# Eight chunks of the modulation as one-column products on TensorE, all in the first block

## The chip, the cores and the metric

One Trainium2 chip, one core of it. The metric is the device time of one execution in microseconds. The five engines (TensorE, VectorE, ScalarE, GpSimd and SyncE) each have their own instruction queue, taken in order, and meet by semaphores. Nearly all plain loads and stores are issued from SyncE's queue.

## What is computed

A streaming-encoder block over 1024 tokens of 1024 channels, in fp32. A vector `c` gives, by one matrix `w_ada` (1024 x 6144), six rows of 1024: shift, scale and gate of each of two sub-layers.

```python
c_act = jax.nn.silu(c)
mod = c_act @ w_ada[l] + b_ada[l]
shift1, scale1, gate1, shift2, scale2, gate2 = jnp.split(mod, 6, axis=-1)
n = modulate(rms_norm(h, g_norm1[l]), shift1, scale1)      # n * (1 + scale) + shift
...                                     # w_in, convolution branch, spatial-gating branch, merged
h = h + gate1[:, None, :] * (merged @ w_out[l])
n2 = modulate(rms_norm(h, g_norm2[l]), shift2, scale2)
h = h + gate2[:, None, :] * peer(n2, w_query[l], sub_keys[l], expert_u[l], expert_v[l])
return rms_norm(h, g_final)
```

`peer` picks 16 of 16384 single-neuron experts for each of 8 heads and each token.

## The kernel before

The 1024 tokens are eight tiles of 128, taken in three blocks of 3, 2 and 3 tiles (`BLOCKS`). For each block `front` (L993) runs the first sub-layer, the second norm and the expert scores. Its products are all of 128 x 128 weights against the block's tokens, in three fp32r passes (high x high, low x high, high x low), so 24 matmuls of 384 columns for a product of the first block. The order in the first block: the loop over eight channel groups with the products `w_av`, `w_ag` (both in `glu`) and `w_u`, and the small mixing products; a loop with `w_gb` and `w_sgu`; a loop with `w_ga`; the convolution's end (L1056); a loop with `w_conv`; then `w_out` (`products_t`), the residual with `gate1`, the second norm and its transposition (`n2_T`, L1098), the next block's `w_v` product (`v_of`) and the query products. Each weight tile of 512 KB is loaded (`raw`), split into a high and a low half by ScalarE and VectorE (`whi`, `wlo`), and the low half is stored to DRAM for the next blocks. The depthwise convolution (31 taps) is a chain of multiply-adds on VectorE, done in the background (`conv`, L899). After the three blocks come the experts, some for all tokens of five tiles as dense products and some by gathered rows.

A planner (`Plan`, L61) writes the order out by hand while the program is built. It keeps an estimated clock for each engine. Between matmul groups `tick` (L263) steps generators whose due time has come: tasks first, then background work by its class. Background work is stepped only while VectorE's clock is less than `lead` ahead of TensorE's, unless it was added with `free=True`. `drain` (L284) steps named generators until they end, wherever TensorE then stands.

The modulation is made in twelve chunks of 512 columns: chunk `ch` is half `ch % 2` of row `ch // 2`. A chunk is four loads of 512 KB (`aw`, a ring of `NST` = 4 buffers shared with `st` tiles that are used much later). Chunks 0 to 3 are made before the first block, half on TensorE (stationary: one column of `cT`, moving: 512 columns of `w_ada`) and half on VectorE. Chunks 4 to 11 are made by `ada` (L742) in the background: eight VectorE operations over 128 partitions into `acc`, one TensorE product with a matrix of ones that adds the partitions and puts the row on all of them, the bias, and for shift2 and scale2 four transposes into `mcol`. The rows go to `rows_d` in DRAM. `rest_of_ada` (L1233) makes three groups of it: (4, 5), gate1; (6, 7, 8, 9), shift2 and scale2; (10, 11), gate2. `front` drains the first at L1073, ahead of the residual, and `n2_T` the first two at L1102, ahead of its transposes. `zeros` (L554) clears 16 MB in DRAM in the same time, a megabyte at a time, when the planner's DMA clock is idle. PSUM has five tiles in `psp` that all products take in turn.

Of the kernel before, what the change touches and what calls it, by code (L numbers as in the profile page):

```python
# [7 lines left out]
F32 = mybir.dt.float32  # L8
# [5 lines left out]
OP = mybir.AluOpType  # L14
AX = mybir.AxisListType

P = 128
D = 1024
J = D // P
# [16 lines left out]
NST = 4  # L36
# [265 lines left out]
def build(ctx, tc, I, O):  # L302
    nc = tc.nc
    out = O["out"]
    pl = Plan(nc)
# [3 lines left out]
    rows_d = dram.tile([4, D], F32, name="rows_d")  # L309
# [13 lines left out]
    ident = cst.tile([P, P], F32, name="ident")  # L323
# [280 lines left out]
    tp = fctx.enter_context(tc.tile_pool(name="tp", bufs=4))  # L604
    sctx = ExitStack()
    gsb = sctx.enter_context(tc.tile_pool(name="gsb", bufs=1, side="right"))
# [3 lines left out]
    def psum():  # L610
        return psp.tile([P, 512], F32, name="ps", tag="ps")

    def cload(name, shape):
        t_ = fc.tile(shape, F32, name=name)
        pl.load(t_, I[name])
        return t_


    def flat(w):
        return w.rearrange("p j c -> p (j c)")  # L620
# [83 lines left out]
    ada_todo = []  # L704
# [30 lines left out]
    cT = cload("cT", [P, J])  # L735
    ones = fc.tile([P, P], F32, name="ones")
    nc.vector.memset(ones, 1.0)
    pl.act(cT, cT, AF.Silu)
    mcol = fc.tile([P, 4, J], F32, name="mcol")


    def ada(ch):  # L742
        which, half = divmod(ch, 2)
        acc = tp.tile([P, 512], F32, name="acc", tag="acc", bufs=3)
        row = tp.tile([P, 512], F32, name="row", tag="acc", bufs=3)
        pl.load(row, I["b_ada"][ch:ch + 1, :].partition_broadcast(P))
        hs = slice(half * 512, (half + 1) * 512)
        raw = []

        def fetch(jq):  # L750
            if jq < 4:
                raw.append(gsb.tile([P, 2, 512], F32, name="aw", tag="st", bufs=NST))
                pl.load(raw[jq], I["w_ada"][ch, jq])

        for jq in range(3):
            fetch(jq)
        for j in range(J):
            w = raw[j // 2]
            yield pl.ready(w)
            if j == 0:  # L760
                pl.ts(acc, w[:, 0, :], cT[:, 0:1], None, OP.mult)
            else:
                pl.stt(acc, w[:, j % 2, :], cT[:, j:j + 1], acc, OP.mult, OP.add)
            if j % 2:
                fetch(j // 2 + 3)
        yield pl.ready(acc)
        ps = psum()
        pl.mm(ps, ones, acc, True, True)
        f = pl.tt(row, row, ps, OP.add)
        yield f  # L770
        if which in (3, 4):
            pt = psum()
            for a in range(4):
                pl.tr(pt[:, a * P:(a + 1) * P], row[:, a * P:(a + 1) * P], ident)
            src = pt.rearrange("p (a b) -> p a b", a=4)[:, :, 0]
            js = slice(half * 4, half * 4 + 4)
            if which == 3:
                pl.vcopy(mcol[:, 2, js], src)
            else:
                pl.stt(mcol[:, 3, js], src, 1.0, cols[:, 6, js], OP.add, OP.mult)  # L780
        if which == 4:
            pl.load(acc, I["g2"][half:half + 1, :].partition_broadcast(P))
            yield pl.ready(acc)
            yield pl.stt(acc, row, 1.0, acc, OP.add, OP.mult)
            pl.load(rows_d[2:3, hs], acc[0:1, :])
        else:
            r = {2: 0, 5: 1, 3: 3}[which]
            pl.load(rows_d[r:r + 1, hs], row[0:1, :])

    held = []  # L790

    def to_T(xn, hi, lo, sl, ca, cb, spill=None):

        while len(held) > 1:
            yield max(pl.now, pl.t["dve"]) + 0.1
        held.append(1)
        nf = tp.tile([P, J, P], F32, name="nf", tag="t4k", bufs=2)
        yield pl.ready(xn)
        for b in range(2):
            pt = psum()  # L800
            for a in range(4):
                j = b * 4 + a
                pl.tr(pt[:, a * P:(a + 1) * P], xn[:, j * P:(j + 1) * P], ident)
            for a in range(4):
                j = b * 4 + a
                src = pt[:, a * P:(a + 1) * P]
                if pl.t["dve"] + DLAG < pl.t["act"]:
                    pl.ts(nf[:, j, :], src, mcol[:, ca, j:j + 1], mcol[:, cb, j:j + 1], OP.mult, OP.add, 1.0)
                else:
                    pl.act(nf[:, j, :], src, AF.Identity, bias=mcol[:, cb, j:j + 1], scale=mcol[:, ca, j:j + 1])  # L810
            js = slice(b * 4, b * 4 + 4)
            f = pl.acopy(hi[:, js, sl], nf[:, js, :])
        yield f
        if spill is not None:
            pl.load(spill, nf)
        f = pl.sub(lo[:, :, sl], nf, hi[:, :, sl].bitcast(F32))
        held.pop()
        yield f

    def norm_tile(x, o):  # L820
        yield pl.ready(x)
        sq = tp.tile([P, D], BF16, name="sq", tag="so", bufs=2)
        ss = tp.tile([P, 1], F32, name="ss", tag="ss")
        yield pl.act(sq, x, AF.Square, accum_out=ss)
        r = tp.tile([P, 1], F32, name="rstd", tag="rstd", bufs=4)
        yield pl.act(r, ss, AF.Sqrt, bias=eps, scale=1.0 / D)
        yield pl.recip(r)
        yield pl.act(o, x, AF.Copy, scale=r)
# [18 lines left out]
    def big(tag, dt=F32):  # L847
        pool = ap if tag[1] in "hl" else ap1
        return pool.tile([P, J, NM], dt, name=tag, tag=tag)
# [143 lines left out]
    def front(b, nn, v, cv):  # L993
# [76 lines left out]
        pl.flush()  # L1070


        pl.drain(ada_todo[:1])  # L1073
        nn = []
        if nxt:
            ng = pl.task(norm_in(*nxt, b + 1, nn))
# [21 lines left out]
        def n2_T(t):  # L1098
            yield pl.ready(h1[:, t, :])
            pl.load(h1_d[tk(t), :], h1[:, t, :])  # L1100
            yield from norm_tile(h1[:, t, :], xn[:, t, :])
            pl.drain(ada_todo[:2])  # L1102
            yield from to_T(xn[:, t, :], n2h, n2l, slice(t * P, (t + 1) * P), 3, 2,
                            n2t_d[:, :, tk(t)] if t0 + t < NDT else None)

# [24 lines left out]
        n2h, n2l = pair(b)  # L1130
        xn = big("sga").rearrange("p j n -> p (j n)").rearrange("p (t d) -> p t d", d=D)
        n2g = [pl.task(n2_T(t)) for t in range(nt)]
        for g in n2g:
            g[3] = -1
# [48 lines left out]
    cols = cload("cols", [P, 9, J])  # L1183
# [7 lines left out]
    f = next(ng)  # L1191

    for tag in ("zc", "sga", "gh", "gl", "nh", "nl"):
        w = big(tag, F32R if tag[1] in "hl" else F32).rearrange("p j n -> p (j n)")
        for a in range(w.shape[1] // D):
            i = len(pieces)
# [11 lines left out]
    for ch in range(4):  # L1208
        acc = tp.tile([P, 512], F32, name="acc", tag="acc", bufs=3)
        ps = psum()  # L1210
        for j in range(J):
            w = pieces[4 * ch + j // 2][:, j % 2 * 512:(j % 2 + 1) * 512]
# [9 lines left out]
        row = tp.tile([P, 512], F32, name="row", tag="acc", bufs=3)  # L1222
# [7 lines left out]
    pl.drain([ng])  # L1230
    v = v_of(*nn, BLOCKS[0][1])

    def rest_of_ada(i, chs):  # L1233
        while any(pl.alive(g) for g in ada_todo[:i]):
            yield pl.now + 1.0
        for ch in chs:
            yield from ada(ch)

    for i, chs in enumerate(((4, 5), (6, 7, 8, 9), (10, 11))):
        ada_todo.append(pl.add(rest_of_ada(i, chs)))  # L1240
    sct = Scatter(gsb, pgp)

    scs = []
# [31 lines left out]
    for b, blk in enumerate(BLOCKS):  # L1275
        nn, v, cv = front(b, nn, v, cv)
# [43 lines left out]
    class Rows:  # L1320
# [7 lines left out]
        def fetch(self):  # L1328
            k = next(self.order, None)
            if k is not None:  # L1330
                self.raw[k] = dq1.tile([P, D], F32, name="raw", tag="raw", bufs=NRAW)
                x, i = k
                pl.load(self.raw[k], flat(I["uT"][i]) if x == "u" else I["v"][i * P:(i + 1) * P, :])
# [132 lines left out]
    for j in range(J):  # L1466
        tag = ("hh", "hl")[j % 2]
# [35 lines left out]
    half = (len(seq) + 1) // 2  # L1503
# [215 lines left out]
```

## Time and profile before

| | us |
|---|---|
| median of 3 runs | 3412.43 |
| lowest and highest | 3403.44, 3421.6 |
| the profiled execution | 3407.5 |
| its span | 3405.0 |

The profile is of one execution, from the hardware's profiler. TensorE's records are its matmuls, and their ends are modelled, so a busy TensorE is not one at its peak; the intervals between starts tell the rate. An fp32 product shows as two matmul records, an fp32r one as one. The granted clock is 1.0 at 2.4 GHz and 0.5 at 1.2 GHz.

### The profile page before, as it was taken

Reading aid. Unit: us, or ns where it says so; the run is one execution under the profiler, and the core shown is the slowest. Engines: PE = TensorE matmul, PEld = TensorE weight load, DVE = VectorE, ACT = ScalarE, POOL = GpSimd, SP = SyncE. Lnnn points to the kernel's source line nnn. Section 1 sums busy time; section 2 is a strip of 40 time slices with the busy share of each in tenths; the row PEclk is TensorE's granted clock in tenths of the full one; section 3 lists DMA queues with packets and bytes.
Section 4 is the critical chain, followed back from the end, with each engine's and each line's share of the span. In section 5 each row is a group of like instructions: output and inputs, shape, how many; then the busy total and the mean of one; then the engine's idle time right before and its main releaser. Section 6 shows DMA issues by size and latency. Waiting matters only on the chain.

```text
span 3405.0 us, 49599 instructions
## 1 busy us (share of the span) xinstructions
PE 3108.5 (91%) x17857; PEld 2831.7 (83%) x17857; DVE 2886.0 (85%) x5888; ACT 1159.3 (34%) x2042; POOL 1471.6 (43%) x1293
## 2 busy tenths in 40 slices
PE   7979858888899989899999999999999999999991
PEld 4969748787799988798999999989999988888980
DVE  4889647777898977659999999989998989999997
ACT  4223433335643365653222222222223222222221
POOL 0000000027899983001555566145514656666663
PEclk9989979999899999899999999999999999999995
DMA  7979678889898877666999999599957999999997
GB/s 249 304 240 308 230 279 291 275 301 287 259 310 233 247 189 244 235 243 200 333 356 337 330 346 361 172 331 340 352 198 284 352 326 350 362 341 358 349 345 272
DMA packets 441830, 997.41 MB, mean 293 GB/s; under 512 B 69384, under 2 KB 212616, under 8 KB 441584
## 3 DMA queue, kind: packets, MB, share of 16 engines
q1 hardware_dynamic: 294000, 591.01, 50.4%
q0 software_dynamic: 147584, 403.24, 34.4%
q8 instruction: 140, 2.29, 0.3%
q14 instruction: 106, 0.87, 0.1%
HBM read 880.32 MB, written 113.79 MB: 292 GB/s over the span
## 4 chain that ended last, share of the span: by engine, by line
PE 53%; DMA 18%; DVE 17%; issue 6%; ACT 3%; POOL 1%; SPq 1%; DVEq 0%; ACTq 0%; POOLq 0%
PE ps L144 18%; PE pa L144 16%; PE pk L144 9%; PE pr L144 6%; PE pg L144 4%; DVE ya L174 4%; DMA raw<-in_v 4%; DMA w<-in_v,e 2%; DVE scr L174 2%; DMA w<-in_u,e 1%; DVE wlo L161 1%; DMA raw<-in_w_out 1%; DVE zc L174 1%; ACT whi L203 1%; DVE vl L161 1%
## 5 line engine op out<-in xcount | busy, mean ns | idle before, releaser
L575 POOL DMA_INDIRECT g_a<-gate,at x256 | 458.7, 1792 | 819.5 <-DVE at L168 744.1
L1420 POOL DMA_INDIRECT w<-in_u,e x384 | 485.7, 1265 | 554.9 <-DVE scr L174 254.3
L1420 POOL DMA_INDIRECT w<-in_v,e x384 | 492.1, 1281 | 336.5 <-DVE ya L174 247.1
L144 PE MATMUL pa<-n2h,uh 128*128 128x320 f32 x2016 | 625.0, 310 | 12.3 <-ACT ge L195 10.1
L144 PE MATMUL pa<-n2l,uh 128*128 128x320 f32 x2016 | 625.4, 310 | 0.8 <-DVE n2l L161 0.8
L144 PE MATMUL pa<-n2h,ul 128*128 128x320 f32 x2016 | 625.0, 310 | 0.0
L174 DVE SCALAR_TENSOR_TENSOR ya<-w,aa,ya 128x1024 f32<-128x1024 f32 x381 | 489.1, 1284 | 27.8 <-DMA w<-in_v,e 22.9
L174 DVE SCALAR_TENSOR_TENSOR scr<-w,n 128x1024 bf16<-128x1024 f32 x384 | 469.6, 1223 | 15.8 <-DMA w<-in_u,e 11.2
L203 ACT CAST whi<-raw 128x1024 fp32r<-128x1024 f32 x264 | 276.7, 1049 | 388.7 <-PE ps L144 90.5
L144 PEld LDWEIGHTS pa<-n2h,uh 128*128 128x128 f32 x2016 | 380.5, 189 | 24.5 <-ACT ge L195 12.6
L144 PE MATMUL ps<-nh,whi 128*128 128x384 f32 (+1 forms) x1024 | 351.5, 343 | 42.8 <-DVE z L161 20.0
L144 PEld LDWEIGHTS pa<-n2l,uh 128*128 128x128 f32 x2016 | 380.5, 189 | 11.1 <-DVE n2l L161 1.7
L144 PEld LDWEIGHTS pa<-n2h,ul 128*128 128x128 f32 x2016 | 380.6, 189 | 0.0
L195 ACT ACTIVATE ge<-pa 128x320 f32<-128x320 f32 x249 | 108.7, 436 | 720.6 <-PE pa L144 720.4
L144 PE MATMUL ps<-nh,wlo 128*128 128x384 f32 (+1 forms) x1024 | 343.7, 336 | 7.9 <-DVE wlo L161 7.7
L144 PE MATMUL ps<-nl,whi 128*128 128x384 f32 (+1 forms) x1024 | 343.0, 335 | 1.6 <-DVE nl L161 1.6
L144 PE MATMUL pk<-vh,hh 128*128 128x512 f32 x768 | 299.5, 390 | 0.0
L144 PE MATMUL pk<-vl,hh 128*128 128x512 f32 x768 | 299.3, 390 | 0.0
L144 PE MATMUL pk<-vh,hl 128*128 128x512 f32 x768 | 299.2, 390 | 0.0
L203 ACT CAST hh<-ge 128x320 fp32r<-128x320 f32 x250 | 115.1, 460 | 509.5 <-DVE ge L161 509.5
L144 PE MATMUL ps<-gh,whi 128*128 128x256 f32 (+1 forms) x704 | 224.2, 318 | 20.5 <-ACT gh L203 17.9
L144 PE MATMUL ps<-gh,wlo 128*128 128x256 f32 (+1 forms) x704 | 219.5, 312 | 18.7 <-DMA wlo<-lo_d_w_ag 12.7
(249 smaller groups left out, 6763.3 us busy)
## 6 DMA issues: line engine op xcount, KB each, us to landing
raw<-in_uT SPq DMA_DIRECT2D x128, 512.0 KB, 6.7
raw<-in_v SPq DMA_DIRECT2D x128, 512.0 KB, 7.1
raw<-in_w_q SPq DMA_DIRECT2D x48, 512.0 KB, 4.2
g_b<-st SPq DMA_DIRECT2D x48, 512.0 KB, 4.7
gt<-g_b SPq DMA_DIRECT2D x32, 640.0 KB, 18.7
wlo<-lo_d_w_q SPq DMA_DIRECT2D x33, 512.0 KB, 6.1
g_a<-zt SPq DMA_DIRECT2D x16, 1024.0 KB, 8.2
aw<-in_w_ada SPq DMA_DIRECT2D x32, 512.0 KB, 7.6
```

What stands on the lines that cost most here:

```text
L144: self.nc.tensor.matmul(ps, w, x, start=start, stop=stop)
L161: self.nc.vector.tensor_tensor(out=out, in0=a, in1=b, op=op)
L174: self.nc.vector.scalar_tensor_tensor(out, a, s, b, op0=op0, op1=op1, **kw)
L195: self.nc.scalar.activation(out, a, func, **kw)
L203: self.nc.scalar.copy(out, a)
L575: i = nc.gpsimd.indirect_dma_start(out=g_1, out_offset=bass.IndirectOffsetOnAxis(ap=at[:, k:k + 1], axis=0), in_=gate[:, k:k + 1], in_offs ...
L1420: nc.gpsimd.indirect_dma_start(out=w, out_offset=None, in_=I["v" if ph else "u"], in_offset=bass.IndirectOffsetOnAxis(ap=ra[a][0][:, k:k + ...
```

## The change

`ada` becomes one generator over all eight chunks, added with `free=True`. The next chunk's four loads are issued when the products of the one before are due to be done. A chunk's eight products run on TensorE as one accumulation into one partition of PSUM, with a column of `cT` stationary; VectorE adds the bias to one partition. The four transposes become four products with a one-element operand into four columns of one PSUM tile. The loads of the bias and of `g2` go to one partition instead of all. `front` drains all chunks at L1073, and the drain in `n2_T` is gone.

```diff
-    def ada(ch):
-        which, half = divmod(ch, 2)
-        acc = tp.tile([P, 512], F32, name="acc", tag="acc", bufs=3)
-        row = tp.tile([P, 512], F32, name="row", tag="acc", bufs=3)
-        pl.load(row, I["b_ada"][ch:ch + 1, :].partition_broadcast(P))
...
-        for jq in range(3):
-            fetch(jq)
-        for j in range(J):
-            w = raw[j // 2]
-            yield pl.ready(w)
-            if j == 0:
-                pl.ts(acc, w[:, 0, :], cT[:, 0:1], None, OP.mult)
-            else:
-                pl.stt(acc, w[:, j % 2, :], cT[:, j:j + 1], acc, OP.mult, OP.add)
-            if j % 2:
-                fetch(j // 2 + 3)
-        yield pl.ready(acc)
-        ps = psum()
-        pl.mm(ps, ones, acc, True, True)
-        f = pl.tt(row, row, ps, OP.add)
...
+    def ada(chs):
+        todo = [(ch, jq) for ch in chs for jq in range(4)]
+        raw = {}
+
+        def fetch():
+            if todo:
+                k = todo.pop(0)
+                raw[k] = gsb.tile([P, 2, 512], F32, name="aw", tag="st", bufs=NST)
+                pl.load(raw[k], I["w_ada"][k])
+
+        for _ in range(4):
+            fetch()
+        for ch in chs:
+            which, half = divmod(ch, 2)
+            hs = slice(half * 512, (half + 1) * 512)
+            row = tp.tile([P, 512], F32, name="row", tag="acc", bufs=3)[0:1, :]
+            pl.load(row, I["b_ada"][ch:ch + 1, :])
+            yield max(pl.ready(raw[ch, 3]), pl.ready(row))
+            ps = psum()
+            for j in range(J):
+                pl.mm(ps[0:1, :], cT[:, j:j + 1], raw[ch, j // 2][:, j % 2, :], j == 0, j == J - 1)
+            yield pl.ready(ps[0:1, :])
+            for _ in range(4):
+                fetch()
+            yield pl.tt(row, row, ps[0:1, :], OP.add)
+            if which in (3, 4):
+                pt = psum()
+                for a in range(4):
+                    pl.mm(pt[:, a:a + 1], row[:, a * P:(a + 1) * P], ones[0:1, 0:1], True, True)
...
+            r = {2: 0, 5: 1, 4: 2, 3: 3}[which]
+            pl.load(rows_d[r:r + 1, hs], row)
...
-        pl.drain(ada_todo[:1])
+        pl.drain(ada_todo)
...
-            pl.drain(ada_todo[:2])
...
-    for i, chs in enumerate(((4, 5), (6, 7, 8, 9), (10, 11))):
-        ada_todo.append(pl.add(rest_of_ada(i, chs)))
+    ada_todo.append(pl.add(ada(range(4, 12)), free=True))
```

## Rows read from the trace of the kernel before

**Rows 1.** The page: engines by busy tenths in 40 equal slices of the span
```profile
PE   7979858888899989899999999999999999999991
DVE  4889647777898977659999999989998989999997
```

**Rows 2.** Busy time by stretch: PE, PEld, DVE, ACT, POOL, granted clock, DMA share, GB/s
```profile
88.00:229.00 141.00, 112.42 (x618) 107.70 (x616) 116.51 (x212) 36.97 (x47) 0.00 (x0) 0.90 0.83 269
229.00:350.00 121.00, 116.13 (x607) 109.88 (x608) 109.27 (x178) 41.87 (x58) 0.00 (x0) 0.96 0.89 289
...
446.00:493.00 47.00, 12.12 (x38) 7.42 (x38) 18.92 (x36) 12.03 (x22) 0.00 (x0) 0.54 0.60 224
493.00:516.00 23.00, 20.71 (x84) 15.86 (x84) 12.22 (x17) 10.22 (x16) 0.00 (x0) 0.98 0.95 354
```

**Rows 3.** TensorE's waits at 88-229, 229-360, 446-493, 516-600: total, times, longest
```profile
PE ps L144 <- DVE z L161: 20.0, 2, 13.4
...
PE ps L144 <- ACT gh L203: 9.2, 1, 9.2
...
PE ps L144 <- DVE acc L174: 32.3, 2, 16.8
...
PE ps L144 <- DMA wlo<-lo_d_w_ag: 5.9, 3, 3.8
```

**Rows 4.** Timeline of TensorE, 445 to 493 us: start, duration, instruction, idle before it
```profile
445.67 0.40 PE L144 MATMUL ps<-whi,gl 128*128 128x512 f32 x1
461.63 2.08 PE L144 MATMUL ps<-acc,ones 128*128 128x512 f32 x2 [15.56 <-DVE acc L174]
...
482.38 2.07 PE L144 MATMUL ps<-acc,ones 128*128 128x512 f32 x2 [16.77 <-DVE acc L174]
...
492.78 0.78 PE L144 MATMUL ps<-whi,gh 128*128 128x512 f32 x1
```

**Rows 5.** Timeline of SyncE's queue: loads of the chunks and of weights
```profile
94.97 1.49 SPq L236 DMA_DIRECT2D aw<-in_w_ada  x3
...
101.60 6.25 SPq L236 DMA_DIRECT2D raw<-in_w_av  x1
...
465.60 0.33 SPq L236 DMA_DIRECT2D raw<-in_w_v  x1
...
468.61 2.13 SPq L236 DMA_DIRECT2D aw<-in_w_ada  x4
...
498.27 0.33 SPq L236 DMA_DIRECT2D raw<-in_w_v  x1
```

**Rows 6.** Timeline of TensorE, 28 to 33 us: products of the first four chunks
```profile
28.90 1.05 PE L144 MATMUL ps<-ones,row 1*128 1x1 f32 x8 [0.66 <-ACT row L203]
29.88 2.73 PE L144 MATMUL ps<-nh,cT 128*1 128x512 f32 x6
```

**Rows 7.** Instructions on tile aw: ns min/median/max, first and last start
```profile
L174 DVE SCALAR_TENSOR_TENSOR acc<-aw,cT,acc x56: 743/752/753, 131.6 to 544.9; 128x512 f32<-128x512 f32 x56
...
L166 DVE TENSOR_SCALAR acc<-aw,cT x8: 478/484/488, 131.0 to 522.7; 128x512 f32<-128x512 f32 x8
...
DMA to landing us min/median/max: 6.9/7.6/8.6
```

**Rows 8.** Timeline of TensorE, 83 to 92 us: first and last of 48 matmuls back to back
```profile
83.77 0.34 PE L144 MATMUL ps<-nh,wlo 128*128 128x384 f32 x1
...
91.92 0.34 PE L144 MATMUL ps<-nl,whi 128*128 128x384 f32 x1
```

**Rows 9.** Groups on TensorE, 88 to 229 us: count, busy us, mean ns, idle before
```profile
L144 PE MATMUL ps<-nh,whi 128*128 128x384 f32 x184 | 65.8, 357 | 25.4 <-DVE z L161 20.0 <-ACT whi L203 3.1 <-ACT ts L195 2.1
```

**Rows 10.** Busy time in ten-microsecond stretches, columns as in rows 2
```profile
100.00:110.00 10.00, 5.76 (x30) 5.12 (x29) 2.23 (x7) 1.44 (x2) 0.00 (x0) 0.92 1.03 356
110.00:120.00 10.00, 10.00 (x48) 10.00 (x48) 8.24 (x14) 2.61 (x3) 0.00 (x0) 0.74 0.91 307
```

**Rows 11.** Timeline of TensorE, 338 to 350 us: the convolution's channel norm
```profile
338.56 5.32 PE L144 MATMUL ps<-zc,onesd 128*128 128x384 f32 x16
```

More of the change, by code (lines that the diff above doesn't have):

```diff
@@ L739, in build @@
     mcol = fc.tile([P, 4, J], F32, name="mcol")
-    def ada(ch):
-        which, half = divmod(ch, 2)
-        acc = tp.tile([P, 512], F32, name="acc", tag="acc", bufs=3)
-        row = tp.tile([P, 512], F32, name="row", tag="acc", bufs=3)
-        pl.load(row, I["b_ada"][ch:ch + 1, :].partition_broadcast(P))
[L747 to L753, printed above, removed]
-        for jq in range(3):
-            fetch(jq)
-        for j in range(J):
-            w = raw[j // 2]
-            yield pl.ready(w)
-            if j == 0:
-                pl.ts(acc, w[:, 0, :], cT[:, 0:1], None, OP.mult)
-            else:
-                pl.stt(acc, w[:, j % 2, :], cT[:, j:j + 1], acc, OP.mult, OP.add)
-            if j % 2:
-                fetch(j // 2 + 3)
-        yield pl.ready(acc)
-        ps = psum()
-        pl.mm(ps, ones, acc, True, True)
-        f = pl.tt(row, row, ps, OP.add)
[L770 to L788, printed above, removed]
@@ new lines, in ada @@
+    def ada(chs):
[25 more added lines that the diff above has]
+                    pl.mm(pt[:, a:a + 1], row[:, a * P:(a + 1) * P], ones[0:1, 0:1], True, True)
+                js = slice(half * 4, half * 4 + 4)
+                yield pl.ready(pt)
+                if which == 3:
+                    pl.vcopy(mcol[:, 2, js], pt[:, 0:4])
+                else:
+                    pl.stt(mcol[:, 3, js], pt[:, 0:4], 1.0, cols[:, 6, js], OP.add, OP.mult)
+            if which == 4:
+                g2 = tp.tile([P, 512], F32, name="g2", tag="acc", bufs=3)[0:1, :]
+                pl.load(g2, I["g2"][half:half + 1, :])
+                yield pl.ready(g2)
+                yield pl.stt(row, row, 1.0, g2, OP.add, OP.mult)
+            r = {2: 0, 5: 1, 4: 2, 3: 3}[which]
+            pl.load(rows_d[r:r + 1, hs], row)
@@ L1231, in build @@
     v = v_of(*nn, BLOCKS[0][1])
[L1233 to L1237, printed above, removed]
-    for i, chs in enumerate(((4, 5), (6, 7, 8, 9), (10, 11))):
-        ada_todo.append(pl.add(rest_of_ada(i, chs)))
+    ada_todo.append(pl.add(ada(range(4, 12)), free=True))
     sct = Scatter(gsb, pgp)
```

## Prediction

> **What bounds the kernel now.** I read from the whole to the part. The page's 40 slices first [rows 1]: TensorE is busy to 9 tenths nearly everywhere, and it ends a slice and a half before VectorE does. The weak slices are the first eighteen; the change lies in the first seven (0 to 600 us). What happens there shifts everything that follows, because the later blocks and the experts depend on this one's output. So the question is by how many microseconds the point at 600 us moves.
>
> Then a table by stretch [rows 2]. The first product loop (88 to 229 us) keeps TensorE busy for 112 of 141 us; 229 to 350 has 116 of 121 and ends in a wait of 9.2 us for the convolution's output [rows 3]; and 446 to 493 has 12 of 47, at a mean granted clock of 0.54. That last hole is the largest on TensorE before the end, and the waits name its cause [rows 3]: 32.3 us in two waits for `acc` on VectorE, which is the modulation itself. The timeline shows it whole [rows 4]: the last `v` product starts at 445.67, then come the `ones` product of chunk 8 at 461.63, that of chunk 9 at 482.38, transposes, and weight products again at 492.78. The drain in `n2_T` (L1102) stands ahead of everything that could fill the hole. VectorE in turn waits for the chunk's loads: those of chunk 9 are issued only at 468.61 [rows 5], because a chunk fetches after the one before has ended. And the next block's `w_v` loads stand behind this on SyncE's queue: one is issued at 465.60, the next at 498.27 [rows 5].
>
> So one part of the old modulation is on the path (chunks 8 and 9), and the rest competes for VectorE and the DMA engines.
>
> **The prices.** A new product (512 columns, fp32, one stationary column) is in the trace already, in the first four chunks: three of them are six records that span 2.73 us from 29.88 [rows 6]. Less the last record's own 0.59, five intervals are 0.428 us each, and a product is two records: 0.856 us. 64 products: 54.8 us of TensorE. The four one-column products that turn a row into columns take 1.05 us per chunk [rows 6]; four chunks: 4 us. Removed from VectorE per chunk: one multiply at 0.48 and seven multiply-adds at 0.75 [rows 7], 5.7 us, 46 us in all. Removed from TensorE: eight `ones` products at 0.856, 7 us, and sixteen small transposes. The add of the bias stays. A weight product's matmul costs 0.173 us: 47 intervals from 83.77 to 91.92 [rows 8].
>
> **First loop, 88 to 229 us (141 us).** It holds 184 x 3 weight matmuls [rows 9], 95.8 us, the small mixing products (eight groups of four of 128 columns, two records each at a quarter of 0.428: 6.8 us) and one `ones` product: 103.5 us of demand, so 37 us are lost now. 20.0 of these are two waits for `z` on VectorE [rows 3], which is behind with the convolution, 5.2 waits for splits and sigmoids [rows 9], the rest half clock (a mean granted clock of 0.90 [rows 2]) and small waits. Afterwards all eight chunks fall here or a little later: a chunk is fetched when the one before is multiplied, so a round is 7 us of products, an issue of four loads at about 0.45 us, and a landing of 6.9 to 8.6 us [rows 7], with the loop's own products running meanwhile: some 20 us, so eight rounds take 160 us and end at 250 to 280. Demand is then 103.5 - 0.9 + 54.8 + 4 = 161 us. The 20 us for `z` go, since VectorE gets 58 us more for the same convolution; about 4 us stay at the start, where SyncE's queue took 1.5 us for three chunk loads and soon after 6.25 us for one `w_av` load [rows 5], and where there are now four chunk loads. New is a wait on TensorE ahead of each chunk's products, which stand in order: the weight products queued behind them wait too, and after them VectorE's splits. The fetch of the next chunk waits on SyncE for these products (the four buffers), and the weight loads, the low-half stores and the zeroing queue behind it. No row shows this wait. Its lower bound is 0 (the loads land in 10 us, while 11 us of other products run), its upper one 6 us (a landing plus such a queue, 8.6 + 6.25, less what runs meanwhile). I take 2.5, nearer the lower end, because the queue's 6 us appear only where loads bunch: 20 us. Together 161 + 4 + 20 = 185 us, **+44** (from +24 with no such wait to +72). The DMA engines bear it narrowly: 141 us at 269 GB/s are 37.9 MB, seven more chunks add 14.7 MB, and 52.6 MB in 185 us are 284 GB/s, where 356 and 307 are reached in busy stretches [rows 10]. At 269 it would be 196 us, +55.
>
> **229 to 360 us (131 us).** 24 products are 99.9 us, the channel norm has two runs of 16 matmul records, about 5.3 us each [rows 11]: 110 of demand. The 9.2 us [rows 3] are the tail of the convolution: its norm starts at 338.56, since VectorE is 90% busy to there [rows 2]. With the convolution two or three channel groups ahead at the end of the first loop, its norm runs beside the products, and the half clock after the hole goes too. What is late next is TensorE itself. I take 116 us, **-15** (-3 to -20; if VectorE is not ahead, only two chunks of multiply-adds leave it).
>
> **360 to 446 us.** Two chunks leave: two `ones` products, eight transposes, and six to eight loads of 512 KB that compete with `w_out`: **-5** (-2 to -8).
>
> **446 to 516 us (70 us).** What must remain: some 80 of the 96 `v` matmuls at 0.23 (0.173 by columns), 18 us, and 24 transposes, 3 us. But about half of the eight `w_v` tiles are still to be loaded, each with its low half, two at a time; a pair takes a landing of 8 us, as for the chunks [rows 7], and a split, about 10 us. So 21 to 40 us, and I take 30: **-40** (-30 to -49). That cost lay under the hole before; it is what is late next.
>
> **516 to 600 us.** Chunk 11 leaves VectorE (5.7 us) and 2 MB leave the DMA engines; 5.9 us of waits for low halves stand here [rows 3]. **-4** (0 to -7).
>
> **After 600 us** nothing of the change is left, but the order written out by the planner shifts; rigid shift, give or take 10 us.
>
> Sum: 44 - 15 - 5 - 40 - 4 = -20 us. The profiled execution took 3407.5 us (span 3405.0); its sum is 3387.5. It lies 4.9 us under the median of the three runs, 3412.43, against which the result is compared: 3392 us, 0.6% less.
>
> **The rivals.** *Waits on TensorE, half clock (slower).* The place is the head of each chunk's eight products. If the loads come 6 us late instead of 2.5, that is 8 x 3.5 = 28 us more. And the clock falls: where TensorE had 4 us of idle time at 100 to 110, the granted clock was 0.92, and 0.74 in the ten microseconds that followed [rows 10], about half of them at 1.2 GHz, 2.6 us lost; eight times 21 us. 3392 + 49 = 3441. It decides from 2.5 us of extra wait per chunk on, without the clock (20 us / 8). For it speaks that DMA is at 0.91 to 1.03 there [rows 10]; against it that TensorE, too, runs late against the plan, which gives the loads the same time. The Trainium skill has this as a rule (TensorE: Matmul & The Clock Gate, "HAM oscillation — how this bites in real kernels"): short bursts of matmuls, each behind a wait for loads, run throttled every time. With all 64 products at half clock that rule alone would add 55 us, by the doubling seen at 461.63 (two records in 2.08 us); by the 29.88 row, taken between load waits at full clock, nothing.
>
> *The hole fills with loads (no difference).* The `w_v`, `h1_d` and `n2t_d` transfers pace 446 to 516, so that only 28 us come back, and the convolution gives 8, not 15: 44 - 8 - 5 - 28 - 4 = -1, 3411 us. For it: DMA at 0.95 in 493 to 516 [rows 2].
>
> *The first loop absorbs more (faster still).* Most of the 37 lost us are reused and no chunk waits: +24, so -40: 3372.
>
> *It does not do what it says.* Chunks are spread past 440 us and the drain, now for all, waits there: the hole stays in part, about 3410. Against it: at 20 us a round they end 160 us earlier.
>
> **How the numbers follow.** Forecast 0.40, first loop absorbs more 0.14, hole fills 0.31, does not do what it says 0.03, waits and half clock 0.12. A measurement of this kernel can tell about 0.5%, 17 us. Faster by more: 0.40 + 0.14 = 0.54; same: 0.31 + 0.03 = 0.34; slower: 0.12. The range reaches up past the no-difference case with the spread of the runs (3403 to 3422), and down to 3364, the absorbing case with 8 us of shift; beyond it lies most of the slower case and a little of the lower bounds.
>
> **What would show it.** Right: no TensorE hole between the last `w_out` product and the next block, SyncE's `w_v` loads without a 30 us gap, eight groups of one-column products all before about 290 us, no wait for `z`, the first loop some 185 us long, the 350 us hole gone. Wrong: waits of over 5 us ahead of these groups with the clock at 0.5, or the first loop beyond 215 us; a hole of over 20 us that stays at the block's end; or later stretches that change by more than 10 us.

## The result and the profile after

| | before | after |
|---|---|---|
| median, us | 3410.48 | 3367.81 |
| lowest and highest | 3403.44 to 3421.6 | 3365.68 to 3371.46 |
| profiled execution and its span | 3407.5, 3405.0 | 3365.68, 3363.9 |

The ratio is 0.9884, with a 95% interval of 0.9867 to 0.9900: 43 us less, clear of noise. The forecast was 20 us less, 3392. The sign and the place were right; the size forecast was less than half of what came.

The page's slices first, TensorE and VectorE, as in [rows 1]:

```profile
PE   7999988897999998999999999999999999999991
...
DVE  3789558787898867669999999989998999998997
```

The third, fifth and sixth slices of TensorE show 9, 9 and 8 where they showed 7, 8 and 5 before; VectorE's first ten have moved by a tenth at most. By stretch, with the columns of [rows 2] and borders moved along with the work:

```profile
88.00:245.00 157.00, 152.43 (x746) 115.51 (x745) 122.18 (x227) 38.57 (x49) 0.00 (x0) 0.99 0.93 320
245.00:370.00 125.00, 124.84 (x644) 108.38 (x642) 104.78 (x169) 48.70 (x67) 0.00 (x0) 1.00 0.83 265
...
447.00:488.00 41.00, 29.91 (x124) 22.92 (x123) 14.78 (x29) 22.96 (x39) 0.00 (x0) 0.92 0.90 329
```

The first loop ends near 245 us, with six of the eight chunks in it (the forecast was 185 us long and held all eight); it has 152 of 157 us busy at a granted clock of 0.99; the next stretch is full at 1.00. The hole of 446 to 493 has become a stretch of 41 us with 30 busy. The whole of TensorE's waits from 88 to 370 us is one row, where [rows 3] had 20.0 for `z` and 9.2 for `gh` (total, times, longest):

```profile
PE ps L144 <- DVE row L161: 4.5, 2, 4.1
```

That is not a wait for loads. It is the four one-column products that follow VectorE's add of the bias. The loads of chunks and their products, SyncE's queue and TensorE's timeline:

```profile
85.07 2.93 SPq L236 DMA_DIRECT2D aw<-in_w_ada  x4
...
265.78 2.96 SPq L236 DMA_DIRECT2D aw<-in_w_ada  x4
```
```profile
94.66 7.03 PE L144 MATMUL ps<-aw,cT 128*1 128x512 f32 x16
...
280.00 7.03 PE L144 MATMUL ps<-aw,cT 128*1 128x512 f32 x16
```

All groups take 7.03 us for 16 records, the price of [rows 6]. The first issue of a chunk's loads stands 9.6 us ahead of the products for the first chunk and 14.2 for the last. A round takes 21 to 34 us, not 20.

How far each point of the program moved, first starts in the two traces:

| point | before | after | moved by | this step | forecast of the step |
|---|---|---|---|---|---|
| first `w_conv` product | 359.68 | 370.52 | +10.8 | +10.8 | +29 |
| first `v` product of the next block | 441.53 | 447.11 | +5.6 | -5.3 | -5 |
| first product of the next block's loop | 516.04 | 487.80 | -28.2 | -33.8 | -40 |
| load of the second block's first `w_u` | 654.85 | 617.38 | -37.5 | -9.2 | -4, to 600 us |
| load of its first `w_gb` | 699.14 | 657.34 | -41.8 | -4.3 | 0 |
| end of the span | 3405.0 | 3363.9 | -41.1 | +0.7 | 0 |

So 18 us of the missing 21 come from the first two stretches, 9.5 from the next block, and the hole gave 6 less than forecast. These are single profiled runs: in a second one of the changed kernel (e15) the next block starts at 492.6 us, 4.8 later.

### The profile page after: what moved, and what is told of

Its sections match the earlier page's. It is cut to its first block, busy times and chain, and to the rows that moved or that the text cites. A ratio compares the mean times of both kernels' runs of the same rounds, so it can differ in the third digit from the quotient of the medians.

```text
span 3363.9 us, 49788 instructions
## 1 busy us (share of the span) xinstructions
PE 3141.7 (93%) x17985; PEld 2830.6 (84%) x17985; DVE 2844.8 (85%) x5829; ACT 1162.1 (35%) x2042; POOL 1468.0 (44%) x1293
## 4 chain that ended last, share of the span: by engine, by line
PE 59%; DVE 15%; DMA 14%; issue 6%; ACT 4%; SPq 1%; POOL 1%; DVEq 0%; ACTq 0%; POOLq 0%
PE ps L144 23%; PE pa L144 16%; PE pk L144 9%; PE pr L144 6%; DMA raw<-in_v 4%; PE pg L144 4%; DVE ya L174 4%; DMA w<-in_v,e 2%; DVE scr L174 2%; DMA raw<-in_w_ag 1%; DMA w<-in_u,e 1%; DVE vl L161 1%; DMA raw<-in_w_q 1%; DVE yb L161 1%; ACT whi L203 1%
## 5 line engine op out<-in xcount | busy, mean ns | idle before, releaser
L144 PE MATMUL pa<-n2h,uh 128*128 128x320 f32 x2016 | 626.2, 311 | 13.7 <-ACT ge L195 11.5
L174 DVE SCALAR_TENSOR_TENSOR ya<-w,aa,ya 128x1024 f32<-128x1024 f32 x381 | 489.1, 1284 | 22.7 <-DMA w<-in_v,e 17.4
L144 PEld LDWEIGHTS pa<-n2l,uh 128*128 128x128 f32 x2016 | 381.5, 189 | 10.8 <-DVE n2l L161 1.4
L144 PE MATMUL ps<-nh,wlo 128*128 128x384 f32 (+1 forms) x1024 | 341.0, 333 | 1.8 <-DVE wlo L161 1.8
L144 PE MATMUL ps<-gh,whi 128*128 128x256 f32 (+1 forms) x704 | 220.6, 313 | 12.3 <-ACT gh L203 11.8
```

What stands on the lines that cost most here:

```text
L144: self.nc.tensor.matmul(ps, w, x, start=start, stop=stop)
L174: self.nc.vector.scalar_tensor_tensor(out, a, s, b, op0=op0, op1=op1, **kw)
```

## The experiments

Kernels of different sessions are compared by their ratios: each is against the kernel before in the same session. A difference of two ratios is given in microseconds by taking it times 3410. "Last group" is the end of the chain of the first block's convolution (its eighth group, VectorE), "next block" the first product of the next block's loop, in the profiled run.

| kernel | median us | ratio, 95% interval | last group | next block |
|---|---|---|---|---|
| before | 3410.48 | 1 | 341.0 | 516.0 |
| changed | 3367.81 | 0.9884 (0.9867 to 0.9900) | 338.5 | 487.8 |
| e1 VectorE, early | 3406.08 | 0.9996 (0.9978 to 1.0014) | 389.8 | 525.5 |
| e2 TensorE, old places | 3381.80 | 0.9913 (0.9878 to 0.9947) | 326.1 | 496.0 |
| e3 products twice | 3412.35 | 1.0017 (0.9997 to 1.0037) | 346.9 | 532.5 |
| e4 one product | 3368.79 | 0.9886 (0.9846 to 0.9925) | 354.6 | 487.3 |
| e5 one load | 3361.62 | 0.9858 (0.9842 to 0.9875) | 323.7 | 477.1 |
| e6 no due time | 3377.50 | 0.9907 (0.9890 to 0.9925) | 350.7 | 493.4 |
| e10 one product, 23 taps | 3344.58 | 0.9815 (0.9791 to 0.9840) | 316.5 | 467.1 |
| e11 23 taps | 3360.70 | 0.9853 (0.9836 to 0.9869) | 281.7 | 482.2 |
| e7 half on VectorE | 3381.18 | 0.9919 (0.9898 to 0.9940) | 357.5 | 497.0 |
| e8 last two late | 3380.54 | 0.9917 (0.9900 to 0.9933) | 343.6 | 483.0 |
| e12 mask on GpSimd | 3520.45 | 1.0326 (1.0307 to 1.0344) | 321.5 | 481.6 |
| e13 e7 and e12 | 3525.89 | 1.0337 (1.0314 to 1.0360) | 338.8 | 480.0 |
| e14 mask on GpSimd, first block | 3359.56 | 0.9859 (0.9838 to 0.9881) | 322.2 | 481.1 |
| e15 changed, same session as e14 | 3365.19 | 0.9882 (0.9860 to 0.9904) | 341.8 | 492.6 |

**Place or engine: e1 and e2.** e1 keeps the old `ada` and places it as the change does:

```diff
-    for i, chs in enumerate(((4, 5), (6, 7, 8, 9), (10, 11))):
-        ada_todo.append(pl.add(rest_of_ada(i, chs)))
+    ada_todo.append(pl.add(rest_of_ada(0, range(4, 12)), free=True))
-        pl.drain(ada_todo[:1])
+        pl.drain(ada_todo)
-            pl.drain(ada_todo[:2])
```

> The old modulation on VectorE, but placed as the change places it: one generator over the eight chunks, stepped first, all drained ahead of the residual, no drain in n2_T. Theory 'place': the gain is the hole of 47 us at the end of the first block, the engine matters little: 3365 to 3380 us. Theory 'engine': VectorE's convolution paces the first block in both kernels (its last group ends at 341.0 us before and 338.5 after), so that the chunks put ahead of it on VectorE (some five more than before in that stretch, 5.7 us each, 30 us) push its end to about 370 and the first w_conv product from 370.5 to about 400: 3390 to 3405 us.

e2 keeps the new `ada` and gives it the old groups and drains:

```diff
-        pl.drain(ada_todo)
+        pl.drain(ada_todo[:1])
+            pl.drain(ada_todo[:2])
+    def rest_of_ada(i, chs):
+        while any(pl.alive(g) for g in ada_todo[:i]):
+            yield pl.now + 1.0
+        yield from ada(chs)
-    ada_todo.append(pl.add(ada(range(4, 12)), free=True))
+    for i, chs in enumerate(((4, 5), (6, 7, 8, 9), (10, 11))):
+        ada_todo.append(pl.add(rest_of_ada(i, chs)))
```

> The new products on TensorE, but in the old places: three groups in the background, the first drained ahead of the residual, the first two in n2_T. Theory 'place': the drain in n2_T waits again, now for the loads of the chunks that are left, about 12 us each: a hole of 25 to 45 us and 3385 to 3410 us. Theory 'engine': without VectorE's multiply-adds the groups end in time by themselves: 3360 to 3375 us, no hole.

e1 gains nothing; its median lies just above the range of theory 'engine'. The hole is gone (the longest wait from 412 to 526 us is 5.5), but VectorE's last group ends 49 us later than before. TensorE's waits from 88 to 412 us:

```profile
PE ps L144 <- DVE z L161: 35.5, 4, 16.1
...
PE ps L144 <- DVE zc L161: 11.1, 1, 11.1
```

The other engine in the old places (e2) gains 0.9% where the change gains 1.2%; its median of 3381.8 lay between the two expectations, and its chunks are done by 427 us, so that neither drain leaves a hole. The early place is thus worth nothing without the other engine, and the engine is worth most of the gain by itself. Whether the early place adds something to it is not shown: the two ratios differ by 10 us, and their intervals overlap.

**Which engine is full: e3, e4, e10, e11.** e3 makes the products twice, e4 makes one of eight:

```diff
-            for j in range(J):
+            for j in [*range(J), *range(J)]:          # e3
+            for j in range(0, J, 8):                  # e4, a sum of its own: True, True
                 pl.mm(ps[0:1, :], cT[:, j:j + 1], raw[ch, j // 2][:, j % 2, :], j == 0, j == J - 1)
```

> The changed kernel with each chunk's eight products made twice (the second set starts the sum anew): 64 more products, 54.8 us more on TensorE, nothing else. If TensorE is full from 94 to 370 us, as its busy time says, the time rises by 45 to 60 us, to 3413 to 3428. If TensorE still waits for loads or for VectorE in places that its modelled ends hide, it rises by less than 30 us.

> The changed kernel with one of each chunk's eight products (seven are left out, so the modulation lacks most of its sum; loads and all the rest stay): 56 products, 48 us less on TensorE. Theory 'TensorE bounds the first block after the change': the first w_conv product comes 35 to 48 us earlier, 3320 to 3335 us. Theory 'VectorE's convolution paces it in both': its end stays near 338 us and the time falls by 0 to 15 us, to 3353 to 3368, with TensorE's idle time back in the first loop.

By ratios, 54.8 us more on TensorE cost 45 against the changed kernel, at the lower edge of the range for a full TensorE; 48 us less gave nothing, with an interval of 13 us to either side and a median just above the range of the theory that VectorE paces. Busy times from 88 to 372 us, e3 and then e4:

```profile
88.00:372.00 284.00, 284.00 (x1247) 186.94 (x1246) 213.66 (x382) 67.99 (x91) 0.00 (x0) 1.00 0.79 252
```
```profile
88.00:372.00 284.00, 242.04 (x1278) 219.92 (x1276) 229.33 (x396) 85.69 (x116) 0.00 (x0) 0.93 0.87 300
```

With one product TensorE has 42 us of idle time again and waits 18.3 us for `z`, and the next block starts when it did (487.3 and 487.8 us). So most of the 48 us left out lie in time that TensorE would lose anyway. One thing came as neither theory had it: the convolution's last group ended at 354.6 us, 16 later than with all products, though VectorE had no more to do. The planner steps background work by its clock for TensorE, which advances less without the products, and it wrote another order: the first group already ended at 159.3 and not 132.2 us. So e4 alone does not tell VectorE's limit from the order that the planner writes, and no run holds the order fixed.

What bounds that time is tested by taking eight of 31 taps out of the first block's convolution, with one product and with all:

```diff
-            for i in range(2, CW - npt):
+            for i in range(2, CW - 8 if k == 1 else CW - npt):
```

> One of eight products per chunk, and the first block's convolution with 23 of its 31 taps (eight taps left out in each of eight groups, 64 operations at 0.53 us start to start, 34 us less on VectorE). With one product alone the time stayed at 3368.8. If VectorE's convolution is what bounded that, the time now falls by 20 to 35 us, to 3334 to 3349. If loads bounded it: 3360 to 3369 us.

> The changed kernel, all products, with 23 of 31 taps in the first block's convolution (eight left out, 34 us less on VectorE). If TensorE and VectorE are both full in the first block after the change, taking from VectorE alone gives little: 3355 to 3366 us. If VectorE alone bounds it, 3334 to 3349 us as with one product.

| ratio, and start of the next block in us | 31 taps | 23 taps |
|---|---|---|
| eight products | 0.9884, 487.8 | 0.9853, 482.2 |
| one product | 0.9886, 487.3 | 0.9815, 467.1 |

By ratios, less TensorE gives 0, less VectorE 11 and both together 24 us, but e4's interval is wide and e11's meets that of the changed kernel at its edge. The start of the next block tells it more clearly: 0.5, 5.6 and 20.7 us earlier, against 4.8 us between two profiled runs of the changed kernel. So in the changed first block two limits stand side by side, TensorE's work and VectorE's queue, and neither alone pays much; how much of VectorE's limit is the planner's order stays open. e10 landed within the range expected for VectorE's bound, e11 within that for two full engines. VectorE's queue is full without being busy all the time: from 88 to 340 us it is busy for 212 of 252 us and stands for 37 in waits, these above all:

```profile
DVE wlo L161 <- ACT whi L203: 17.9, 9, 4.6
DVE ws L832 <- DMA ws<-in_ws: 17.4, 4, 5.4
```

The second row is VectorE waiting for the loads of the mixing tables (`ws`).

**The wait that was forecast: e5 and e6.** e5 leaves out three of a chunk's four loads, e6 the planner's due time:

```diff
-        todo = [(ch, jq) for ch in chs for jq in range(4)]
+        todo = [(ch, 0) for ch in chs]                            # e5, and one fetch() for four
-            yield max(pl.ready(raw[ch, 3]), pl.ready(row))
+            yield                                                 # e6
```

> The changed kernel with one of each chunk's four loads (three are left out, 12.6 MB; all eight products read the one tile, so the modulation is another sum). The prediction put 20 us on products that wait for their loads; the trace after shows no such wait. If loads cost the first block nothing: 3368 plus or minus 5 us. If they cost it indirectly, because VectorE waits for weight tiles and mixing tables behind them (35 us in 88 to 340 us): 3350 to 3360 us, with these waits halved and the convolution's last group before 330 us.

> The changed kernel without the planner's due time for a chunk: its products are put into TensorE's queue right behind the issue of their loads. Theory 'the due time hides the loads': now every chunk's products stand in order and wait 5 to 9 us for the landing, eight times, all of the queue with them: 3400 to 3430 us. Theory 'TensorE runs late by itself' (the queue is so far behind the plan that loads land in time anyway): 3365 to 3378 us.

e6 lies within the range of the second theory: TensorE runs late by itself. Shown are its waits for the chunks' loads, two groups on its timeline (the first chunk and the third), and VectorE's largest wait in total from 88 to 340 us:

```profile
PE ps L144 <- DMA aw<-in_w_ada: 8.0, 2, 6.9
```
```profile
90.96 8.84 PE L144 MATMUL ps<-aw,cT 128*1 128x512 f32 x16 [6.95 <-DMA aw<-in_w_ada]
...
110.38 7.03 PE L144 MATMUL ps<-aw,cT 128*1 128x512 f32 x16
```
```profile
DVE row L161 <- PE ps L144: 33.4, 4, 9.2
```

Only two of the eight groups wait for loads, the first for 6.95 us and the last for 1.05; the other six find theirs landed, though nothing holds the products back. The chunks are done by 192.6 instead of 286.4 us, in rounds of 9 to 21 us. By ratios the kernel loses 8 us against the changed one, and not by these waits alone: VectorE stands for 33.4 us in its queue until TensorE has made the products to which it adds the bias, a wait that does not show after the change, and the convolution's last group ends 12 us later. Behind the one long wait the clock was at its lower level for a while: the first group's 16 records took 8.84 us and not 7.03, at a granted clock of 0.67 from 88 to 98 us. The mean of 88 to 340 us is still 0.99.

e5 lies between its two expectations, 6 us below the changed kernel by medians and 9 by ratios, and the intervals overlap. In its profiled run, the fastest of the four, the last group ends 15 us earlier, and VectorE's waits for mixing tables are 6.0 us and not 17.4. So the chunks' loads may cost a little through VectorE; TensorE's waits for them are 0.3 us.

**Late chunks: e8.** Chunks 10 and 11 by the old VectorE code, released at the next block's `v_of`:

```diff
-    ada_todo.append(pl.add(ada(range(4, 12)), free=True))
+    ada_todo.append(pl.add(ada(range(4, 10)), free=True))
+    pl.add(last_two())       # waits for the first block's end, then ada_v(10), ada_v(11): the old ada
```

> The changed kernel with chunks 10 and 11 made as before the change, by VectorE in the background after the first block's end; the other six by TensorE. The stretch from the next block's first product to the expert stage took 995.7 us before and 981.1 after, and 981 to 987 in all kernels without late chunks. If the two late chunks cost that stretch 10 to 14 us (VectorE, their loads), it returns to 991 to 996 and the time is 3376 to 3384; if the difference is the planner's other order, it stays under 988 and the time is 3360 to 3372.

The time was as expected for late chunks that cost, the stretch was not: from the next block's first product to the expert stage 1010 us, more than before. The number of chunks is not the reason. Chunk 10's eight operations on VectorE start at 469.65 to 480.63 us, ahead of the next block's first product at 482.98; behind it lie seven multiply-adds of chunk 11, as many as before the change behind 516.04. Yet from that product to the load of the second block's first `w_u` it is 138.8 us before, 129.6 changed and 154.2 in e8 (482.98 to 637.17). TensorE's waits from 483 to 620 us and VectorE's from 483 to 637 us in e8:

```profile
PE ps L144 <- DMA wlo<-lo_d_w_ag: 9.6, 3, 3.5
PE ps L144 <- ACT qT L203: 7.6, 2, 4.0
```
```profile
DVE row L161 <- PE ps L144: 9.8, 2, 8.3
```

Before, the last of these rows had 0.2 us in this stretch. In e8 VectorE stands 8.3 us in its queue until TensorE takes chunk 11's `ones` product at 590.86, which itself is behind a wait for `qT` in TensorE's queue. So e8 shows what a late chunk can do by its place in two queues; it gives no price of a chunk.

**A faster version: e7, e12, e13, e14.** e7 gives VectorE half of each chunk again:

```diff
-            for j in range(J):
-                pl.mm(ps[0:1, :], cT[:, j:j + 1], raw[ch, j // 2][:, j % 2, :], j == 0, j == J - 1)
+            for j in range(0, J, 2):
+                pl.mm(ps[0:1, :], cT[:, j:j + 1], raw[ch, j // 2][:, 0, :], j == 0, False)
+            ...                    # odd j: ts, stt into acc on VectorE, a yield after each
+            pl.mm(ps[0:1, :], ones[:, 0:1], acc, False, True)
```

> The changed kernel with four of each chunk's eight products on TensorE, four as multiply-adds on VectorE, and a ninth product that adds the partitions, as the first four chunks are made before the first block. TensorE loses 24 products, 20 us; VectorE gets 32 operations, 23 us. If TensorE is the tighter of the two: 3350 to 3360 us. If VectorE's convolution is (one product alone gave nothing, eight taps less gave 7 us): 3380 to 3392 us.

By ratios it is 12 us slower than the changed kernel, within the range for VectorE's bound: VectorE is the worse place for half a chunk. e12 moves the zeroing of each mixing table's corner to GpSimd, e13 does both:

```diff
-            nc.vector.memset(w[64:128, 0:64], 0.0)
+            nc.gpsimd.memset(w[64:128, 0:64], 0.0)
```

> The changed kernel with one small operation moved: the zeroing of the upper corner of each mixing table, on VectorE, is made by GpSimd, which is idle then. VectorE stood 17.4 us in four waits for these tables' loads in 88 to 340 us. If such waits are part of what paces the convolution: 3355 to 3364 us, no more, since TensorE is full there. If not: 3365 to 3371.

> Both at once: half of each chunk on VectorE, and the mask's zeroing on GpSimd. TensorE loses 20 us, VectorE gets 23 us of work and loses up to 17 us of waits. If the two engines share the bound, it ends within 8 us of the changed kernel, 3360 to 3376; if TensorE alone bounds, 3345 to 3355.

Both miss by 150 us, and not in the first block: there the next block's first product came 6 to 8 us earlier. From 692 us on, behind the second block's memsets, GpSimd's queue holds scatters, and the third block's memsets stand between them. A table whose load was issued at 1008.37 us was cleared at 1134.21, and TensorE stood for it. TensorE's largest wait in total from 600 to 1300 us in e12, then GpSimd's and TensorE's timelines:

```profile
PE ps L144 <- POOL ws L832: 180.3, 8, 118.9
```
```profile
1132.61 1.56 POOL L575 DMA_INDIRECT g_a<-gate,at  x1 [0.18 <-issue]
1134.21 0.23 POOL L832 MEMSET ws<- 64x64 f32 x2
```
```profile
1134.41 1.65 PE L144 MATMUL ps<-ws,v 128*128 128x128 f32 x6 [118.94 <-POOL ws L832]
```

e14 does it in the first block alone, with the changed kernel (e15) beside it:

> The changed kernel with the mask's zeroing on GpSimd in the first block alone, and on VectorE in the other two, where GpSimd's queue is full of scatters. With the mask on GpSimd everywhere the next block's first product came at 481.6 us, not 487.8, and the 180 us of waits came only later. If VectorE's in-order waits for the mixing tables are part of what paces the first block: 4 to 9 us less than the changed kernel of the same session. If the 6 us were chance: within 3 us of it.

> The changed kernel once more, as the measure for the one above in the same session: 3362 to 3374 us, 0.985 to 0.990 of the kernel before.

VectorE's waits for the tables are gone there, its last group ends at 322 instead of 342 us, and the next block starts 11.5 us earlier. By the load of the second block's first `w_gb` 9.8 are left, by the expert stage (1471.4 and 1475.8) 4.4. The medians differ by 5.6 us, in the expected band, but the ratios' intervals overlap: by its end time e14 is not told apart from the changed kernel, only by its first block.

## Why the prediction was right and wrong

**Right: the hole.** The drain's hole of [rows 4] is gone, and what is late next are the `w_v` tiles, as forecast. TensorE's timeline, 450 to 490 us:

```profile
454.38 0.80 PE L144 MATMUL ps<-wlo,gh 128*128 128x512 f32 x1 [4.08 <-DMA wlo<-lo_d_w_v]
...
466.52 1.09 PE L154 MATMUL ps<-ident,sga 128*128 128x128 f32 x8 [2.05 <-ACT sga L195]
...
477.99 0.60 PE L144 MATMUL ps<-wlo,gh 128*128 128x512 f32 x1 [3.41 <-DMA wlo<-lo_d_w_v]
```

The term was -40; the step measured -33.8. From the first `v` product on it took 40.7 us, where the forecast comes to 34.5: there are three waits of 2 to 4 us, two of them for loads, and the granted clock of 447 to 488 us was 0.92. The 360 to 446 us term (-5) measured -5.3.

**Wrong by size: the wait ahead of each chunk's products.** This is the step that failed. It stood in the sum with 20 us, as 8 x 2.5, and with 4 more at the start. Both measured 0. Without the 20 us the first two terms are +24 and -15, +9 in sum, where +10.8 was measured, and the forecast is 3372, where 3367.8 was measured. This is the rival "the first loop absorbs more", which had a chance of 0.14. The lower bound, "the loads land in 10 us, while 11 us of other products run", was the right end, and the prediction had the reason in its case against the slower rival: TensorE "runs late against the plan, which gives the loads the same time". e6 shows it: without the due time six of eight groups still find their loads landed, and the waits are 8.0 us in all. With the due time they are 0, and a round is 21 to 34 us long. What was left of TensorE's lost time were 4.5 us for the bias add, which the prediction did not name.

**Wrong in its reason: the convolution.** The prediction had VectorE get "58 us more for the same convolution", which was to be "two or three channel groups ahead" at the end of the first loop. It was not ahead: four of its eight groups were done there in both kernels (the fourth at 227.8 and 236.4 us), and the last ended at 338.5 instead of 341.0. Only two of the old chunks, 11 us of work, lay on VectorE before 340 us. From 88 to 340 us its busy time fell from 220.5 to 212.0 us, and its waits rose from 29.5 to 37.2. TensorE's waits for the convolution went all the same, as forecast, because the new products fill the time in which TensorE used to wait (e4, e10, e11). The effect was right; the reason was not.

**Wrong by size: the next block.** Chunk 11 was priced at 4 us, by its 5.7 us on VectorE and 2 MB. The stretch took 138.8 us before and 129.6 after, and TensorE's waits in it add up to 18.0 and 12.3 us. In all fourteen profiled kernels without a late chunk the stretch took 129.0 to 134.0 us. So 5 to 10 us went. That chunk 11 alone made them is not shown, since e8 took 154.2 with as much of it.

**Partly luck: the total.** That the sum without the 20 us comes within 5 us of the result is partly luck: the hole gave 6.2 us less than forecast and the next block 9.5 more.

**Open.** Of the remaining 4.3 us, between the second block's first `w_u` and `w_gb` loads (44.3 us before, 40.0 after), no run shows a cause; e8 has 40.0 too, so a late chunk is not enough for it.

The rival with half clock did not come: the granted clock was 0.99 in 88 to 245 us, and no chunk waited for loads. The rule of the Trainium skill named there (TensorE: Matmul & The Clock Gate, "HAM oscillation — how this bites in real kernels") is about bursts that each stand behind a wait for loads. The one group that did, the first of e6, agrees with it: 6.95 us of wait, then 1.8 us lost at the lower clock. The row of 29.88 us that the prediction sets against it stands behind a wait for ScalarE [rows 6] and not for loads.

## What to carry to other kernels

Ask of added work not how long it is, but how much of it fits into time that its engine loses to a neighbour anyway: here 55 us of products moved the block by 11 us, and the next 55 us cost 45. Test such a balance by taking work from each engine alone and from both; where two limits stand side by side, the pair pays much more than either. Price a wait for loads from the moment at which the engine reaches the work, late as it may be, and not from the issue of the loads. And a small operation should not be moved to an engine that is idle now if its queue is full later in the program.

## What was not expected of the hardware

Products with a single stationary column, 128 records in eight groups of 16, ran at 0.43 us from start to start, in stretches whose granted clock was 0.99 and 1.00. And one 64 x 64 memset of 0.15 us on GpSimd, in order behind scatters, held TensorE for up to 118.9 us.
